# Three RMS norms of an encoder layer rearranged: ones as the stationary operand in halves, squares summed elsewhere, operands made in pieces

## The chip, the core and the metric

The kernel runs on one core of a Trainium2 chip. Five engines work at the same time, each on its own instructions in order: TensorE (PE in the profile; PEld is its loading of weights), VectorE (DVE), ScalarE (ACT), GpSimd (POOL) and SyncE (SP), which here mostly issues DMAs. SBUF holds the tiles, PSUM the results of matmuls, and an instruction waits on semaphores for what it reads or overwrites. The metric is the device time of one execution in microseconds (us), as the median over runs.

## The reference

One layer of a streaming encoder for a prompt of 512 tokens and eight decode streams of 16 tokens (640 columns together, model width 2048). RMS norms stand at four places; the change touches the first and the two inside `merge_and_ffn`.

```python
def rmsnorm(x, g):
    xf = x.astype(jnp.float32)
    y = xf * lax.rsqrt(jnp.mean(xf * xf, axis=-1, keepdims=True) + EPS)
    return (y * g.astype(jnp.float32)).astype(x.dtype)
...
def merge_and_ffn(x, oa, ob, norm_grp_a, norm_grp_b, w_out, norm_ffn, w_gate, w_up, w_down):
    o = jnp.concatenate([rmsnorm(oa, norm_grp_a), rmsnorm(ob, norm_grp_b)], axis=-1)
    x = x + o @ w_out
    h = rmsnorm(x, norm_ffn)
    return x + (jax.nn.silu(h @ w_gate) * (h @ w_up)) @ w_down
...
    qa, ka, va, qb, kb, vb = split_proj(rmsnorm(x, norm_mix) @ w_in)
```

Group A (`oa`) is chunk-band attention of 16 heads of 64 with a learned bias and keys of 8 earlier chunks; group B (`ob`) is sliding-window attention with sinks and rotary keys. Each group's result is 1024 wide and has a norm of its own ahead of its half of `w_out`.

## The kernel before

Activations lie transposed: features on the 128 partitions, the 640 tokens along the row, in two halves of HT = 320. The 2048 features are KT = 16 tiles, a group's result 8 tiles (512 prompt columns, SP in the code, and 128 of decode). A product in fp32 accuracy is made of three matmuls in fp32r (`mm3`, L235 to L237): each operand is split into a high part, written by ACT (L226 for weights, L230 for activations with the norm's gain), and the rest, written by DVE (L227, L231). One `dense` (L247) makes one tile of 128 outputs: for each input tile the two halves times three matmuls, into one pair of PSUM banks (`dn`). Other PSUM results (scores, transposes, sums of norms) take banks from the pool `at`.

A norm's factor depends on the token alone, so it is applied to the result of the product: DVE multiplies the PSUM result by `r_mix` (L412), `r_b` (L1004) or `r_a`. These tiles are 128 x 640 with the same row on every partition. `rstd_steps` (L265) makes them from `ssq`, the sum over tiles of squares: PE sums over the partitions with `ssq` as the stationary operand and a column of ones as the moving one (L273, six columns in all, one for each block of up to 128 tokens), DVE and ACT work out 1/sqrt with a Newton step on 128 x 6 numbers (L275 to L280, ACT's square root with its table at L276), and after a yield PE spreads them over the partitions again (L285, six matmuls against the identity); ACT copies them out of PSUM (L290).

The program's order, as far as the change touches it:
- The start loads `xT` tile by tile with the first pieces of `w_in` (START_CHUNKS) on SP's queue. The gains of the norms come second there (L373) and are read by the first split_gain (L230).
- `input_norm` squares all 16 input tiles on ACT (L389), adds them on DVE (L394), and then runs `rstd_steps`. It runs as a queue beside the first two `dense`, a step at a time as matmuls are emitted; L412 then frees the first `dn` pair.
- Next come group B's heads, and the projections for q, k and v as quartets of Strassen products. In the last quartet (to about 536 us) `release` loads the eight tiles of `ob` and makes group B's operands from them (split_gain), as input tiles become free.
- Then `w_out_b`: 16 `dense` of 8 input tiles, m = 0 to 15. Their matmuls share PE with three queues that the helper `pump` serves in turns: the norm (`norm_b`: seven squares on ACT L302 after a first at L299, added on DVE L303, then `rstd_steps`), group A's heads (scores L425 to L428, exponentials L438, weighted values L464), and the decode of group A (`decode_a`). Once m = 1 is emitted, the norm's queue is run out and `r_b` used. At m = 12 what is left of the queues is run out.
- Group A's results go to memory (`oa_d`) as they are made (`done`, and L730 for decode). `group_operands` (L917) loads them again, splits them, squares them on ACT and adds the squares on POOL: four tiles at m = 12, four after m = 15. Its `rstd` stands behind the first `dense` of `w_out_a`.

Tiles come from lists that are handed on by hand (`get`, `put`), so a tile that is put back earlier or later also moves who waits for it.

## Time and profile before

| what | us |
|---|---|
| runs: median (lowest to highest) | 2544.72 (2541.51 to 2547.5) |
| the profiled execution, whole | 2540.53 |
| its span, first to last instruction | 2538.8 |
| PE busy | 2488.2 |
| DVE busy | 1966.8 |
| ACT busy | 1057.6 |
| POOL busy | 703.2 |

The mean granted TensorE clock is 0.995. An overview by 40 equal slices of some 63 us each; a digit is the busy share in tenths, 9 is 90% or more, and PEclk is the granted clock in tenths of the full one:

```profile
PE   8999999989999999999999999999999999999997
DVE  6666767685567787788888888888889877777797
ACT  5445333355555544344343334334334333333343
POOL 0001211110021133323332332323335433333453
PEclk9999999999999999999999999999999999999998
DMA  6234433467863434444344334334437765666655
```

The first slice holds the start and the input norm, the ninth and tenth (508 to 635 us) the end of the quartets and group B's norm, the twelfth and thirteenth group A's norm and `w_out_a`, and everything after that the feed-forward part, which the change leaves alone.

### The profile page before, as it was taken

What the parts mean: (1) busy time and instruction counts of PE and PEld (TensorE: products, weight loads), DVE (VectorE), ACT (ScalarE), POOL (GpSimd) and SP (SyncE); (2) the same over time, 40 slices, a digit from 0 to 9 for tenths busy, and PEclk for the clock granted to TensorE, in tenths of its full rate; (3) what the DMA queues carried; (4) which work ended last, traced back from release to release, by engine and by line L of the source; (5) the groups of instructions that cost most, each with busy time, mean ns of one, the idle gap of its engine ahead of it and who ended that gap; (6) DMA issues with size and microseconds to landing.
All of it is one profiled execution on the core that took longest, in us unless ns stands there. A gap on an engine that the chain in (4) does not pass through costs nothing.

```text
span 2538.8 us, 44665 instructions
## 1 busy us (share of the span) xinstructions
PE 2488.2 (98%) x17325; PEld 2422.5 (95%) x17325; DVE 1966.8 (77%) x2930; ACT 1057.6 (42%) x1701; POOL 703.2 (28%) x566
## 2 busy tenths in 40 slices
PE   8999999989999999999999999999999999999997
PEld 8898899988899999999999999999999999999997
DVE  6666767685567787788888888888889877777797
ACT  5445333355555544344343334334334333333343
POOL 0001211110021133323332332323335433333453
PEclk9999999999999999999999999999999999999998
DMA  6234433467863434444344334334437765666655
GB/s 197 83 98 131 148 123 127 135 235 244 263 219 139 140 130 138 149 156 134 128 130 146 120 127 144 133 128 131 145 120 247 249 170 165 182 171 172 186 160 183
DMA packets 191604, 401.68 MB, mean 158 GB/s; under 512 B 22496, under 2 KB 83936, under 8 KB 191392
## 3 DMA queue, kind: packets, MB, share of 16 engines
q1 hardware_dynamic: 167056, 344.75, 41.5%
q0 software_dynamic: 23184, 52.77, 7.6%
q8 instruction: 136, 2.23, 0.4%
q10 hardware_dynamic: 1152, 1.31, 0.2%
q14 instruction: 76, 0.62, 0.1%
HBM read 311.14 MB, written 86.87 MB: 157 GB/s over the span
## 4 chain that ended last, share of the span: by engine, by line
PE 87%; DVE 7%; DMA 2%; issue 1%; ACT 1%; POOL 0%; SPq 0%; DVEq 0%; ACTq 0%; POOLq 0%
PE dn L235 18%; PE dn L237 17%; PE dn L236 17%; PE at L235 10%; PE at L236 10%; PE at L237 10%; DVE W L227 2%; PE at L341 2%; PE at L464 1%; DMA W<-w_in 1%; PE at L425 1%; DVE S L793 1%; DMA W<-xT 1%; PE at L713 0%; ACT W L226 0%
## 5 line engine op out<-in xcount | busy, mean ns | idle before, releaser
L226 ACT ACTIVATE W<-W 128x1024 fp32r<-128x1024 f32 (+2 forms) x662 | 640.0, 968 | 1050.5 <-PE dn L236 554.9
L235 PE MATMUL dn<-S,W 128*128 128x320 f32 x3374 | 1055.9, 313 | 10.3 <-ACT W L226 5.1
L237 PE MATMUL dn<-S,W 128*128 128x320 f32 x3374 | 1046.3, 310 | 7.9 <-DVE W L227 7.7
L236 PE MATMUL dn<-S,W 128*128 128x320 f32 x3374 | 1044.7, 310 | 0.3 <-DVE S L227 0.3
L227 DVE TENSOR_TENSOR W<-W,W 128x1024 fp32r<-128x1024 f32 (+2 forms) x662 | 798.0, 1206 | 89.7 <-ACT W L226 85.5
L235 PEld LDWEIGHTS dn<-S,W 128*128 128x128 f32 x3374 | 635.0, 188 | 27.1 <-issue 13.8
L237 PEld LDWEIGHTS dn<-S,W 128*128 128x128 f32 x3374 | 634.4, 188 | 13.4 <-DVE W L227 11.7
L236 PEld LDWEIGHTS dn<-S,W 128*128 128x128 f32 x3374 | 635.1, 188 | 1.1 <-DVE S L227 0.6
L237 PE MATMUL at<-S,W 128*128 128x320 f32 x1834 | 567.4, 309 | 1.2 <-DVE W L227 1.0
L235 PE MATMUL at<-S,W 128*128 128x320 f32 x1834 | 567.6, 309 | 0.9 <-ACT W L226 0.9
L236 PE MATMUL at<-S,W 128*128 128x320 f32 x1834 | 567.0, 309 | 0.0
L774 POOL TENSOR_TENSOR W<-W,W 128x1024 f32<-128x1024 f32 (+2 forms) x84 | 181.3, 2158 | 771.9 <-DVE W L227 617.7
L237 PEld LDWEIGHTS at<-S,W 128*128 128x128 f32 x1834 | 344.5, 188 | 2.2 <-DVE W L227 1.9
L235 PEld LDWEIGHTS at<-S,W 128*128 128x128 f32 x1834 | 344.7, 188 | 1.4 <-ACT W L226 1.4
L236 PEld LDWEIGHTS at<-S,W 128*128 128x128 f32 x1834 | 344.7, 188 | 0.0
L793 DVE TENSOR_TENSOR S<-S,dn 128x320 f32<-128x320 f32 x398 | 182.2, 480 | 76.2 <-PE dn L237 75.7
L783 POOL TENSOR_TENSOR W<-W,W 128x1024 f32<-128x1024 f32 (+2 forms) x84 | 186.5, 2220 | 182.7 <-DVE W L227 136.4
L793 DVE TENSOR_TENSOR S<-S,at 128x320 f32<-128x320 f32 x292 | 138.3, 482 | 96.4 <-PE at L237 94.8
L767 DVE TENSOR_TENSOR W<-W,W 128x1024 f32<-128x1024 f32 (+2 forms) x86 | 119.9, 1394 | 37.7 <-DMA W<-w_gate 26.1
L771 DVE TENSOR_TENSOR W<-W,W 128x1024 f32<-128x1024 f32 (+2 forms) x86 | 97.9, 1139 | 59.1 <-DMA W<-w_up 29.4
L1082 POOL DMA_DIRECT2D S<-act_d x161 | 88.0, 547 | 166.7 <-PE dn L237 80.1
L1146 DVE TENSOR_TENSOR S<-S,half 128x320 fp32r<-128x320 f32 x147 | 119.8, 835 | 1.9
(157 smaller groups left out, 1703.2 us busy)
## 6 DMA issues: line engine op xcount, KB each, us to landing
S<-act_d POOLq DMA_DIRECT2D x161, 320.0 KB, 3.9
W<-w_gate SPq DMA_DIRECT2D x88, 512.0 KB
W<-w_up SPq DMA_DIRECT2D x88, 512.0 KB
W<-w_in SPq DMA_DIRECT2D x66, 512.0 KB
W<-w_down SPq DMA_DIRECT2D x64, 384.0 KB
act_d<-half SPq DMA_DIRECT2D x147, 160.0 KB
act_d<-S SPq DMA_DIRECT2D x147, 160.0 KB
W<-w_down SPq DMA_DIRECT2D x68, 320.0 KB
```

The lines of the kernel that those rows point to most:

```text
L226: self.nc.scalar.activation(hi, src, AF.Identity)
L227: self.nc.vector.tensor_tensor(lo, src, f(hi), ALU.subtract)
L235: mm(out, a[0], b[0], start=first, stop=False)
L236: mm(out, a[0], b[1], start=False, stop=False)
L237: mm(out, a[1], b[0], start=False, stop=last)
L767: nc.vector.tensor_tensor(b12[:, w], b12[:, w], b22[:, w], sub)
L771: nc.vector.tensor_tensor(s6[:, w], b11[:, w], b12[:, w], sub)
L774: eng.tensor_tensor(b11[:, w], b22[:, w], s6[:, w], sub)
L783: eng.tensor_tensor(b21[:, w], b21[:, w], s6[:, w], sub)
L793: add = lambda o, a, b: nc.vector.tensor_tensor(o, a, b, ALU.add)
L1082: nc.gpsimd.dma_start(out=r(sh(t, 2, HT)), in_=r(act_d[which, :, j]))
L1146: nc.vector.tensor_tensor(r(src), src, hi, ALU.subtract)
```

## The change

1. *Start.* The gains are loaded from ACT's own DMA queue as its first instruction, and a small activation on the ones (made by a memset on POOL) stands ahead of all other ACT work. SP loses that issue.
2. *`wide_steps`* takes the place of `rstd_steps` in the input norm and in group B's. PE now has the ones, broadcast to 128 x 128, as the stationary operand and each half of `ssq` as the moving one, so the sum stands on all partitions at once; DVE takes it from PSUM with scale and EPS, ACT makes the square root of 128 x 640, and DVE the reciprocal and the Newton step on two halves of 320 columns. The second visit to PE and ACT's copies are gone.
3. *Group B.* `release` has ACT square each tile of `ob` in place, right behind its split_gain; `norm_b` only adds the eight on DVE.
4. *Group A.* `done` squares each head pair's 512 prompt columns on ACT and adds them on POOL; `sum_decoded` squares the decode columns on ACT, two yields behind their store, and adds them on DVE. `group_operands` makes no squares and runs at m = 12, 13 and 14 for three, three and two tiles; `rstd` follows at m = 14. On PE its first matmul stands 96 matmuls sooner than before, and 25 matmuls instead of 22 stand between its two visits.

```diff
...
+    def wide_steps(self, ssq, dim, out):
+        nc = self.nc
+        tmp = self.get("S")
+        for a in range(2):
+            ps, half = self.bank()[:, :HT], ssq[:, a * HT:a * HT + HT]
+            nc.tensor.matmul(ps, self.ones.to_broadcast([P, P]), half, start=True, stop=True)
+            nc.vector.tensor_scalar(half, ps, 1.0 / dim, EPS, ALU.mult, ALU.add)
+        yield
+        nc.scalar.activation(tmp, ssq, AF.Sqrt)
+        for a in range(2):
+            y, t, v = (x[:, a * HT:a * HT + HT] for x in (out, tmp, ssq))
+            nc.vector.reciprocal(y, t)
+            nc.vector.tensor_tensor(t, y, y, ALU.mult)
+            nc.vector.scalar_tensor_tensor(t, t, -0.5, v, ALU.mult, ALU.mult)
+            nc.vector.scalar_tensor_tensor(y, t, 1.5, y, ALU.add, ALU.mult)
+            yield
+        self.put("S", tmp)
...
-            sq = self.get(lst)
+            own = self.get(lst)
+            sq = own[:, :x.shape[-1]]
             nc.scalar.activation(sq, x, AF.Square)
             (eng or nc.gpsimd).tensor_tensor(ssq, ssq, sq, ALU.add)
-            self.put(lst, sq)
+            self.put(lst, own)
...
     n.ident, mask_b, n.ones = cst[:, :P], cst[:, P:], gains[:, rest:]
+    nc.scalar.dma_start(out=gains[:, :rest], in_=io["consts"][:, P + 257:])
     nc.gpsimd.memset(n.ones, 1.0)
+    nc.scalar.activation(n.small(1), n.ones, AF.Identity)
...
         xr = n.get("S")
         dma(out=xr, in_=io["xT"][:, kt])
-        if kt == 0:
-            dma(out=gains[:, :rest], in_=io["consts"][:, P + 257:])
...
-        for _ in n.rstd_steps({a: [xs[0][:, a * HT:a * HT + HT]] for a in range(2)}, D, r_mix):
-            for _ in range(3):
+        n.put("S", xs[1])
+        for _ in n.wide_steps(xs[0], D, r_mix):
+            for _ in range(2):
                 yield
-        n.put("S", xs[0], xs[1])
+        n.put("S", xs[0])
...
+    ssq_a, summed = [], set()
+    def sum_decoded(o):
+        nc.scalar.activation(o[:, :512], o[:, :512], AF.Square)
+        nc.vector.tensor_tensor(o[:, :256], o[:, :256], o[:, 256:512], ALU.add)
+        out = ssq_a[0][:, SP:]
+        if SP in summed:
+            nc.vector.tensor_tensor(out, out, o[:, :P], ALU.add)
+            nc.vector.tensor_tensor(out, out, o[:, P:2 * P], ALU.add)
+        else:
+            nc.vector.tensor_tensor(out, o[:, :P], o[:, P:2 * P], ALU.add)
+        summed.add(SP)
     def heads_of(kind, p, held, *args):
         def done(ot):
             dma(out=(oa_d if kind is prompt_a else ob_d)[p, :, :SP], in_=ot[:, :SP])
+            if kind is prompt_a:
+                n.add_square(ssq_a[0][:, :SP], ot[:, :SP], 0 not in summed, "S")
+                summed.add(0)
             n.put("S", ot)
...
         dma(out=oa_d[4 * g:4 * g + 4, :, SP:].rearrange("t p c -> p t c"), in_=sh(o_s, 4, P))
-        n.put("W", *three)
+        n.put("W", *three[1:])
+        yield
+        yield
+        sum_decoded(three[0])
+        n.put("W", three[0])
...
-    def group_operands(o_d, gain, ssq, tiles):
+    def group_operands(o_d, gain, tiles):
         own, out = [], []
         for t in tiles:
             o = n.get("S")
             dma(out=o, in_=o_d[t])
             two, hl = pair("S")
             n.split_gain(o, gain[:, t:t + 1], *hl)
-            n.add_square(ssq, o, t == 0, "S")
...
             n.split_gain(raw_b[t], g_b[:, t:t + 1], *hl)
+            nc.scalar.activation(raw_b[t], raw_b[t], AF.Square)
...
     def norm_b():
-        ssq = n.get("S")
-        for t, o in enumerate(raw_b):
-            n.add_square(ssq, o, t == 0, "S", nc.vector)
-            n.put("S", o)
-            yield
-        for _ in n.rstd_steps({a: [ssq[:, a * HT:a * HT + HT]] for a in range(2)}, 1024, r_b):
-            yield
-        n.put("S", ssq)
+        ssq = raw_b[0]
+        for t in range(1, 8):
+            add(ssq, ssq, raw_b[t])
+            if t % 3 == 0:
+                yield
+        yield
+        for _ in n.wide_steps(ssq, 1024, r_b):
+            yield
+        n.put("S", *raw_b)
...
-    r_a, ssq_a, ssq = n.get("S"), n.get("S"), n.get("S")
+    r_a, ssq = n.get("S"), n.get("S")
+    ssq_a.append(n.get("S"))
+    own_a, acts_a = [], []
...
         if m == 12:
             n.drain()
-            own_a, acts_a = group_operands(oa_d, g_a, ssq_a, range(4))
+        if m >= 12:
+            own, out = group_operands(oa_d, g_a, range(3 * (m - 12), min(3 * (m - 12) + 3, 8)))
+            own_a.extend(own)
+            acts_a.extend(out)
+        if m == 14:
+            n.rstd(ssq_a[0], 1024, r_a)
     n.put("S", r_b, *own_b)
-    more = group_operands(oa_d, g_a, ssq_a, range(4, 8))
-    own_a, acts_a = own_a + more[0], acts_a + more[1]
...
-        if i == 0:
-            n.rstd(ssq_a, 1024, r_a)
...
```

The rows below are the order of one engine's instructions in the built program: line, operation, written tile <- read tiles (tile names with a running number), shape. First, the start. SP before, where `gains` stand second and the first 768-column piece of `w_in` behind `cst`:

```order
L371 DMA S_6_84<-xT 128x640
L373 DMA gains<-consts 128x82
L241 DMA W_7_87<-w_in 128x256
L371 DMA S_12_97<-xT 128x640
L241 DMA W_13_99<-w_in 128x256
L371 DMA S_18_109<-xT 128x640
L371 DMA S_24_121<-xT 128x640
L378 DMA cst<-consts 128x128
L379 DMA cst<-consts 128x256
L371 DMA S_27_129<-xT 128x640
L241 DMA W_19_111<-w_in 128x768
L241 DMA W_28_131<-w_in 128x768
```

SP after, with `gains` gone from it and the first 768-column piece ahead of `cst` and the fifth `xT` tile:

```order
L393 DMA S_7_87<-xT 128x640
L241 DMA W_8_89<-w_in 128x256
L393 DMA S_13_99<-xT 128x640
L241 DMA W_14_101<-w_in 128x256
L393 DMA S_19_111<-xT 128x640
L393 DMA S_25_123<-xT 128x640
L241 DMA W_20_113<-w_in 128x768
L398 DMA cst<-consts 128x128
L399 DMA cst<-consts 128x256
L393 DMA S_28_131<-xT 128x640
L241 DMA W_29_133<-w_in 128x768
```

ACT at the same place, before; its first work waits for the gains:

```order
L230 ACT_TABLE_LOAD
L230 ACTIVATE S_10_93<-S_6_84,gains 128x640
L226 ACTIVATE S_8_88<-W_7_87 128x256
L226 ACTIVATE S_14_100<-W_13_99 128x256
L230 ACTIVATE S_16_105<-S_12_97,gains 128x640
L230 ACTIVATE S_22_117<-S_18_109,gains 128x640
```

ACT after, where the table load stands behind the DMA issue, with the small activation on the ones:

```order
L353 DMA gains<-consts 128x82
L355 ACT_TABLE_LOAD
L355 ACTIVATE sm_76<-gains 128x1
L230 ACTIVATE S_11_95<-S_7_87,gains 128x640
L226 ACTIVATE S_9_90<-W_8_89 128x256
L230 ACTIVATE S_17_107<-S_13_99,gains 128x640
L226 ACTIVATE S_15_102<-W_14_101 128x256
L409 ACTIVATE S_7_87<-S_7_87 128x640
```

The table load now belongs to an activation that reads no loaded data.

Second, ACT in the last quartet. S_798 to S_805 before, and S_796 to S_803 after, are the eight tiles of `ob`; L230 is the gain split of one, L226 the split of a quartet's weights. Before:

```order
L226 ACTIVATE W_816_5389<-W_814_5386 128x1024
L230 ACTIVATE S_812_5381<-S_799_5332,gains 128x640
L230 ACTIVATE S_818_5417<-S_800_5334,gains 128x640
L230 ACTIVATE S_820_5421<-S_801_5336,gains 128x640
L230 ACTIVATE S_824_5455<-S_802_5338,gains 128x640
L226 ACTIVATE W_822_5427<-W_791_5266 128x1024
L230 ACTIVATE S_826_5459<-S_803_5340,gains 128x640
L230 ACTIVATE S_831_5494<-S_804_5342,gains 128x640
L226 ACTIVATE W_829_5466<-W_814_5386 128x1024
L226 ACTIVATE W_855_5531<-W_790_5264 128x1024
```

After, with the squares in place (L988) between them:

```order
L226 ACTIVATE W_814_5383<-W_812_5380 128x1024
L230 ACTIVATE S_810_5374<-S_797_5324,gains 128x640
L988 ACTIVATE S_796_5322<-S_796_5322 128x640
L230 ACTIVATE S_816_5411<-S_798_5326,gains 128x640
L230 ACTIVATE S_818_5416<-S_799_5328,gains 128x640
L988 ACTIVATE S_797_5324<-S_797_5324 128x640
L988 ACTIVATE S_798_5326<-S_798_5326 128x640
L226 ACTIVATE W_820_5423<-W_789_5258 128x1024
L988 ACTIVATE S_799_5328<-S_799_5328 128x640
L230 ACTIVATE S_822_5451<-S_800_5330,gains 128x640
L230 ACTIVATE S_824_5456<-S_801_5332,gains 128x640
L226 ACTIVATE W_827_5464<-W_812_5380 128x1024
```

Three squares now stand ahead of the split W_820, and a fourth ahead of W_827. Each square overwrites a tile that DVE's L231 still reads, so it waits for that.

Third, group B's norm, on ACT and PE. ACT before, up to the split of the third block of `w_out_b` (W_955), which stands 30 rows behind that of the second:

```order
L438 ACTIVATE S_852_5527,sm_5838<-S_852_5527,sm_5837 128x128
L438 ACTIVATE S_853_5528,sm_5838<-S_853_5528,sm_5837 128x256
L438 ACTIVATE S_853_5528,sm_5838<-S_853_5528,sm_5837 128x384
L438 ACTIVATE S_852_5527,sm_5838<-S_852_5527,sm_5837 128x512
L573 ACTIVATE S_921_5849<-at_5850 128x512
L573 ACTIVATE S_923_5862<-at_5863 128x512
L673 ACTIVATE S_930_5890,sm_5887<-S_929_5889,sm_5886 128x256
L674 ACTIVATE S_930_5890,sm_5888<-S_929_5889,sm_5886 128x16
L454 ACTIVATE S_946_5946<-at_5941 128x512
L454 ACTIVATE S_948_5959<-at_5954 128x512
L226 ACTIVATE W_955_5975<-W_954_5974 128x1024
```

ACT after, from the split of the second block (W_899) to that of the third (W_948): one head's four exponentials (L459) and two copies stand between them, and one square root with its table.

```order
L226 ACTIVATE W_899_5760<-W_898_5759 128x1024
L301 ACT_TABLE_LOAD
L301 ACTIVATE S_883_5666<-S_796_5322 128x640
L459 ACT_TABLE_LOAD
L459 ACTIVATE S_841_5517,sm_5713<-S_841_5517,sm_5712 128x128
L459 ACTIVATE S_842_5518,sm_5713<-S_842_5518,sm_5712 128x256
L459 ACTIVATE S_842_5518,sm_5713<-S_842_5518,sm_5712 128x384
L459 ACTIVATE S_841_5517,sm_5713<-S_841_5517,sm_5712 128x512
L611 ACTIVATE W_870_5611<-at_5746 128x512
L611 ACTIVATE W_879_5657<-at_5787 128x512
L226 ACTIVATE W_948_5969<-W_947_5968 128x1024
```

PE before, around the first visit of the norm, in the `dense` of m = 1 (`dn_5742`); the second visit (L285) stands 28 rows behind:

```order
L235 MATMUL dn_5742<-S_810_5377,W_903_5744 128x320
L236 MATMUL dn_5742<-S_811_5378,W_903_5744 128x320
L237 MATMUL dn_5742<-S_810_5377,W_904_5745 128x320
L273 MATMUL at_5755<-gains,S_871_5601 128x1 x6
L341 MATMUL at_5775<-cst,S_876_5615 128x128 x4
L235 MATMUL dn_5742<-S_812_5381,W_903_5744 128x320
L236 MATMUL dn_5742<-S_813_5382,W_903_5744 128x320
L237 MATMUL dn_5742<-S_812_5381,W_904_5745 128x320
```

PE after, where the norm's only visit (L298) stands in the `dense` of m = 0, ahead of four score matmuls (L446):

```order
L298 MATMUL at_5667<-S_796_5322,gains 128x320
L298 MATMUL at_5670<-S_796_5322,gains 128x320
L235 MATMUL dn_5576<-S_822_5451,W_863_5578 128x320
L236 MATMUL dn_5576<-S_823_5452,W_863_5578 128x320
L237 MATMUL dn_5576<-S_822_5451,W_864_5579 128x320
L235 MATMUL dn_5576<-S_822_5451,W_863_5578 128x320
L236 MATMUL dn_5576<-S_823_5452,W_863_5578 128x320
L237 MATMUL dn_5576<-S_822_5451,W_864_5579 128x320
L446 MATMUL at_5679<-S_836_5507,S_837_5508 128x256
L446 MATMUL at_5680<-S_836_5507,S_837_5508 128x256
L446 MATMUL at_5685<-S_831_5497,S_832_5498 128x256
L446 MATMUL at_5686<-S_831_5497,S_832_5498 128x256
```

The norm's first work on PE moved up by 34 rows.

More of the change, by code (lines that the diff above doesn't have):

```diff
@@ L1068, in build @@
                 pass
-    n.put("S", r_a, ssq_a, *own_a)
+    n.put("S", r_a, *ssq_a, *own_a)
     n.move("WH", "H", 4)
```

## The prediction

> **What bounds the kernel now.** I read the page first: the busy times, then the chain that ended last by engine.
>
> ```profile
> PE 2488.2 (98%) x17325; PEld 2422.5 (95%) x17325; DVE 1966.8 (77%) x2930; ACT 1057.6 (42%) x1701; POOL 703.2 (28%) x566
> PE 87%; DVE 7%; DMA 2%; issue 1%; ACT 1%; POOL 0%; SPq 0%; DVEq 0%; ACTq 0%; POOLq 0%
> ```
>
> The matmul engine PE is busy for 2488.2 of 2538.8 us, so no more than some 50 us of idle time can be taken out of it, and the rest of a gain must be matmuls that go away. A change to VectorE (DVE) or ScalarE (ACT) pays only where PE waits for them. So I went by stage: busy time in 40-us windows, at the start, around group B's norm (500 to 620) and around group A's (700 to 780). Columns: stretch, length, PE, weight loads, DVE, ACT, POOL, granted clock, DMA share, GB/s.
>
> ```profile
> 0.00:40.00 40.00, 31.64 (x193) 30.23 (x194) 31.42 (x38) 30.67 (x43) 3.01 (x9) 1.00 0.82 261
> 500.00:540.00 40.00, 38.76 (x258) 37.07 (x258) 31.93 (x39) 22.29 (x28) 8.71 (x8) 1.00 0.72 240
> 540.00:580.00 40.00, 34.23 (x247) 30.09 (x250) 25.97 (x89) 22.87 (x60) 4.22 (x11) 0.91 0.62 212
> 740.00:780.00 40.00, 40.00 (x281) 40.00 (x280) 21.00 (x29) 15.17 (x22) 5.35 (x3) 1.00 0.55 182
> ```
>
> Three of the change's places hold idle PE time; group A's norm holds none (40.00 of 40.00). There only PE's own work counts, and that is the same on both sides: squares and operands that are ready sooner end no wait.
>
> **Term 1, the start.** The timeline of the first 16 us:
>
> ```profile
> 0.74 0.40 SPq L371 DMA_DIRECT2D S<-xT  x1
> 1.20 0.41 SPq L373 DMA_DIRECT2D gains<-consts  x1
> 1.65 0.43 SPq L241 DMA_DIRECT2D W<-w_in  x1
> 4.00 1.28 ACT L230 ACT_TABLE_LOAD   x1 [4.00 <-DMA gains<-consts]
> 5.29 0.83 ACT L230 ACTIVATE S<-S,gains 128x640 fp32r<-128x640 f32 x1
> 6.03 0.40 ACT L226 ACTIVATE S<-W 128x256 fp32r<-128x256 f32 x1
> 6.48 0.63 PE L235 MATMUL dn<-S,S 128*128 128x320 f32 x1 [6.48 <-ACT S L226]
> 8.20 0.63 PE L235 MATMUL dn<-S,S 128*128 128x320 f32 x1 [1.09 <-ACT S L226]
> 14.87 0.41 PE L237 MATMUL dn<-S,W 128*128 128x320 f32 x1 [0.62 <-DVE W L227]
> ```
>
> The table load stands on the path only because it waits for the gains. With the dummy activation on the ones it runs from about 1 us and is gone from the path: L230 starts when the gains and xT[0] are in. The gains landed 2.8 us after their issue (1.20 to 4.00); issued first on ACT's queue at about 0.8 they land near 3.6, and xT[0], issued by SP at 0.74, by the same 2.8 about then. L230 then starts near 3.75 instead of 5.29, and the first matmul near 5.0 to 5.2 instead of 6.48: about 1.4. On SP each issue behind the gains moves up by 0.45 (1.20 to 1.65), and the first 768-column chunk passes three issues of some 0.45 each (cst twice and xT[4]); the 0.62 before 14.87 was DVE splitting that chunk late. Together 1.8. Bounds: 0.5 (only the SP issue moves, if data set the pace: DMA share 0.82) to 2.6 (1.28 of table load, 0.62, and 0.7 of the 1.09).
>
> **Term 2, PE's own work in two norms.** The chain of waits at the input norm and at group B's:
>
> ```profile
> 55.99 1.23 PE at L273 x12
> 59.97 1.28 PE at L285 x12
> 554.12 1.23 PE at L273 x12
> 559.66 1.28 PE at L285 x12
> ```
>
> Before, a norm is two visits to PE: six one-column sums (1.23), and six spreading matmuls of 640 columns in all (1.28). After, it is one visit of two 128x320 f32 matmuls, again 640 columns; I take 1.28 for it. Each norm so loses 1.2 of PE work: 2.4 for two. Bounds: 0.8 to 1.4 for each.
>
> At the input norm the wide chain must not be late. PSUM's bank pair is freed by L412, which needs r_mix.
>
> ```profile
> 61.29 0.44 ACT L290 ACTIVATE S<-at 128x320 f32<-128x320 f32 x1 [0.23 <-PE at L285]
> 63.24 0.82 DVE L412 SCALAR_TENSOR_TENSOR S<-dn,S 128x640 f32<-128x640 f32 x1
> 70.92 1.07 ACT W L226
> L277 DVE RECIPROCAL sm<-sm 128x6 f32<-128x6 f32 x4 | 0.7, 187 | 0.3 <-ACT sm L276 0.3
> L678 DVE RECIPROCAL sm<-sm 128x1 f32<-128x1 f32 x16 | 2.5, 159 | 0.2
> L793 DVE TENSOR_TENSOR S<-S,dn 128x320 f32<-128x320 f32 x398 | 182.2, 480 | 76.2 <-PE dn L237 75.7
> ```
>
> No row has a reciprocal of 320 columns. Its low bound is any 320-wide row, 0.48; from 1 to 6 columns the time goes from 159 to 187 ns, 5.6 ns per column, so 320 columns are about 2.0. I take 2.0, as an estimate from the reciprocal's own rows; eight times the per-column price of a 640-wide add (0.82 of L412's kind) would be 3.3, the high bound. Two reciprocals and six plain operations are then 2 x 2.0 + 6 x 0.48 = 6.9 (3.8 to 9.5), behind two PSUM reads of 0.48 and a square root with its table (1.28, and 0.83 like L230). With one PE visit and two ACT copies gone, r_mix comes near 63 instead of 61.7, and L412 ends 2 to 4 later than its 64.06. The next dense is not done before 70.9, so these 7 us cover it: no cost.
>
> The Trainium skill speaks against the wide form: "VectorE: DVE Perf Modes", in its part on the resources of a lane, says that the reciprocal is an iterative divide with a repeat count of 8. At the page's 0.96 GHz that would be about 2.7 us for 320 columns (an estimate from that page), so the chain would take 8.3; the cover above takes it too, so the sum would be the same. No trace here has the wide form yet.
>
> **Term 3, group B's norm and the stalls around it.** PE's gaps there, each with what ended it:
>
> ```profile
> 525.73 0.41 PE L237 MATMUL dn<-S,W 128*128 128x320 f32 x1 [1.24 <-DVE W L227]
> 545.89 0.91 PE L425 MATMUL at<-S,S 64*128 64x256 f32 x4 [0.69 <-DVE sm L428]
> 548.00 1.43 PE L425 MATMUL at<-S,S 64*128 64x256 f32 x4 [1.21 <-DVE sm L428]
> 569.58 0.41 PE L235 MATMUL dn<-S,W 128*128 128x320 f32 x1 [2.50 <-ACT W L226]
> 571.51 0.42 PE L237 MATMUL dn<-S,W 128*128 128x320 f32 x1 [1.38 <-DVE W L227]
> ...
> 548.00:552.00 4.00, 4.00 (x15) 3.35 (x16) 3.90 (x19) 1.61 (x7) 0.42 (x2) 0.57 0.96 348
> 572.00:576.00 4.00, 4.00 (x21) 3.96 (x20) 1.23 (x1) 1.92 (x4) 0.00 (x0) 0.57 0.76 256
> ```
>
> That is 7.0 us of idling, and after the second and the last gap the granted clock falls to 0.57 of full speed over 4 us, 1.7 lost each: up to 3.4. I count 2.5, since some of it falls on short operations. In all 9.5.
>
> What the change does to them, from the order of ACT and DVE:
> - The seven L303 adds leave DVE's stretch of 535 to 549, where they alternate with the score pass L428 for which PE waits (four of 0.81 stand between 542 and 549). The two gaps before 545.89 and 548.00 shrink; but PE's new L298 pair stands between the scores and needs banks from the same pool. Left of 1.9: about 1.8 (0 to 2.5), in two waits.
> - The 2.50 and the 1.38 are one chain: the split L226 of the third w_out_b block stands on ACT behind four heads' exponentials, norm B's two tables and its copies. After, it stands behind one head's; both gaps go.
> - New: ACT's squares in place, in the last quartet. Each must wait until DVE's L231 has read the same tile, and ACT works in order, so the split L226 behind it waits as well:
>
> ```profile
> 519.51 3.83 DVE L231 SCALAR_TENSOR_TENSOR S<-S,gains,S 128x640 fp32r<-128x640 f32 x2
> 523.66 0.87 DVE L231 SCALAR_TENSOR_TENSOR S<-S,gains,S 128x640 fp32r<-128x640 f32 x1
> 520.89 1.04 ACT L226 ACTIVATE W<-W 128x1024 fp32r<-128x1024 f32 x1
> 533.59 4.49 ACT L302 ACTIVATE S<-S 128x640 f32<-128x640 f32 x7
> ```
>
> Those two L231 end at 523.3, and two squares (0.64 each, 4.49 by 7) follow: the split of 520.89 moves to about 524, and PE's gap of 1.24 becomes about 2.0. Bounds: 1.0, if the DVE runs the two earlier, and 4.
>
> Left in the stage: 2.0 + 1.8, and 0.7 for a chance of 4 in 10 of one clock fall of 1.7: 4.5. Term 3 is 4.5 - 9.5 = -5.0 (-8 to 0).
>
> By the Trainium skill, "TensorE: Matmul & The Clock Gate", Part 1, the clock is halved after at least one idle window of about 3.4 us. The rows differ: gaps of 1.21 and of 2.50 with 1.38 were followed by 0.57. By that rule a new gap of 2.0 costs nothing more, and the stage would be 0.7 better; I go by the rows.
>
> **Term 4, group A.** Eight ACT squares of 128x512, POOL adds and the decode squares are spread over 580 to 735, where PE is nearly full:
>
> ```profile
> 580.00:620.00 40.00, 39.46 (x400) 30.83 (x388) 24.04 (x94) 17.91 (x54) 3.65 (x15) 1.00 0.78 265
> 700.00:740.00 40.00, 39.54 (x322) 35.22 (x320) 31.22 (x75) 28.23 (x64) 9.47 (x5) 1.00 0.62 203
> ```
>
> DVE has 24 and 31 of 40 us to do, so they hide mostly; what stands behind a decode square on ACT waits for the store of group A's decoded rows with it, about 1 us once. I take +0.7 (0 to 3); if the cover of the weights read ahead were gone, each square would cost its 0.6. The three pieces of operands at m = 12 to 14 fall into a stretch with PE full, and rstd at 14 comes 96 matmuls sooner than before, with 25 matmuls of cover against 22.
>
> **The sum.** -1.8 - 2.4 - 5.0 + 0.7 = -8.5, against the profiled execution's own 2540.53: 2532.0. That execution lies 4.2 below the median of the runs, 2544.72, so the forecast is 2536.2, called **2536**.
>
> **The rivals.**
> 1. *Given back in place*, about 2541: the stalls of norm B only move. For it: DVE and ACT are fullest just there (31.93 and 22.29 of 40), so a gap taken from one wait finds the next engine late. Then term 3 is 0 and the others give -3.5. Against it: the split moves ahead of three heads' work.
> 2. *The slower side: ACT held behind squares.* All eight squares wait for a slow L231 (1.9), not two of them. Four weight splits of the last quartet stand behind them; each then comes 2.5 late, and each gap may take a clock fall of 1.7 with it: 4 x 4.2 = 16.8 in place of the 2.0 that I count. That is -8.5 + 14.8 = +6.3, or 2551. It decides from about three late splits on (3 x 4.2 = 12.6 against 2.0 + 8.5). Against it: the next L231, at 523.66, took 0.87.
> 3. *The start is set by data.* The first weights and xT land when they land (share 0.82 over 40 us), and term 1 is 0.5: 2537.5; inside the range.
> 4. *More goes*: one wait of 1.5 is all that remains in the stage, and term 1 is full: -2.4 - 8 - 2.6 = -13, or 2531.7.
> 5. *The change doesn't do what it says* for group A: the order shows rstd earlier, yet no wait ends by it. This is in the forecast, whose time it leaves.
>
> **How the numbers follow.** Forecast (with 3) 0.52, rival 1 0.25, rival 2 0.10, rival 4 0.13. A measurement of this kernel can't tell less than 0.2%, 5.1 us, from no change: the line lies at 2539.6. Faster: 0.13 + 0.48 of the forecast's 0.52 + 0.05 = 0.66; slower: 0.07 of rival 2; the same: 0.27. The terms' bounds all at their best give -2.6 - 2.8 - 8 = -13.4, or 2531; all at their worst -0.5 - 1.6 - 0 + 3 = +0.9, or 2546. Below, I add the 3 us by which a run lay off the median; above, rival 2 is left out, with 1 in 10. Range 2528 to 2546.
>
> **What would show it.** First matmul near 5.1 and L227's gap gone near 13 us; two L298 matmuls of some 1.3 us together in each norm, no L273 there; reciprocals of 320 columns at 2.0; no wait for L226 of over 1 us at 565 to 575; a gap of about 2.0 near 524 to 527; PE full at 740 to 780 as before. The forecast falls if several gaps over 1.2 stand between 515 and 540, if the granted clock in 540 to 580 stays at 0.91, or if r_b, late from reciprocals over 2.7, holds L1049 (before L1004).

## The result, and the profile after

| | before | changed |
|---|---|---|
| median of 7 runs, us | 2543.25 | 2535.75 |
| lowest to highest | 2541.51 to 2547.5 | 2531.67 to 2537.58 |
| profiled execution's span | 2538.8 | 2534.9 |

The ratio is 0.9967 (95% interval 0.9956 to 0.9979): 7.5 us faster by the medians, against 8.5 forecast. The two profiled spans differ by only 3.9; where the rest hides is said in the explanation.

The windows of the changed kernel, with the columns of those before:

```profile
0.00:40.00 40.00, 33.19 (x200) 32.11 (x201) 31.92 (x39) 31.66 (x45) 3.57 (x10) 1.00 0.82 265
500.00:540.00 40.00, 38.29 (x248) 37.58 (x246) 31.17 (x37) 22.76 (x28) 7.87 (x7) 0.96 0.69 229
540.00:580.00 40.00, 37.83 (x314) 32.25 (x315) 34.45 (x107) 25.65 (x70) 5.29 (x13) 1.00 0.69 233
740.00:780.00 40.00, 40.00 (x281) 40.00 (x280) 20.66 (x32) 15.69 (x23) 3.48 (x2) 1.00 0.46 155
```

PE gains 1.6 us of work in the first window and 3.6 in the third, where the granted clock went from 0.91 to 1.00; in the second it fell from 1.00 to 0.96. PE is full at 740 to 780, as before.

The timeline at the start of the changed kernel (start, duration, engine, line; in brackets the idle time before and what ended it):

```profile
1.18 1.28 ACT L355 ACT_TABLE_LOAD   x1 [1.18 <-PEq L1453]
4.30 0.83 ACT L230 ACTIVATE S<-S,gains 128x640 fp32r<-128x640 f32 x1 [1.62 <-DMA gains<-consts]
5.49 0.63 PE L235 MATMUL dn<-S,S 128*128 128x320 f32 x1 [5.49 <-ACT S L226]
15.03 0.84 ACT L226 ACTIVATE W<-W 128x768 fp32r<-128x768 f32 x1 [1.08 <-DMA W<-w_in]
15.93 0.41 PE L235 MATMUL dn<-S,W 128*128 128x320 f32 x1 [1.33 <-ACT W L226]
```

The table load is gone from the path and PE starts 1.0 sooner. At 15.93 it waits 1.33 for the second 768-column piece, whose split starts at 15.03; before it started at 14.95. The gains still come only at 4.30, though they are issued first.

The wide form: first the reciprocals as a group (count, total in us, mean in ns), then PE and DVE at the input norm and PE's gaps around group B's, from the timeline:

```profile
L304 DVE RECIPROCAL S<-S 128x320 f32<-128x320 f32 x4 | 8.3, 2117 | 0.8 <-ACT S L301 0.8
```

```profile
54.77 1.24 PE L298 MATMUL at<-S,gains 128*128 128x320 f32 x4
66.38 0.82 DVE L433 SCALAR_TENSOR_TENSOR S<-dn,S 128x640 f32<-128x640 f32 x1
...
525.78 0.42 PE L235 MATMUL dn<-S,W 128*128 128x320 f32 x1 [0.92 <-ACT W L226]
527.12 0.42 PE L237 MATMUL dn<-S,W 128*128 128x320 f32 x1 [0.79 <-DVE W L227]
548.35 1.34 PE L298 MATMUL at<-S,gains 128*128 128x320 f32 x4 [1.40 <-DVE sm L449]
550.87 1.49 PE L446 MATMUL at<-S,S 64*128 64x256 f32 x7 [0.30 <-DVE sm L449]
565.45 0.30 PE L363 MATMUL at<-cst,S 128*128 128x128 f32 x1 [0.48 <-DVE S L466]
```

From 525.78 on, these are all of PE's gaps of 0.3 us and more between 500 and 600. The 2.50 and the 1.38 are gone. The gap ahead of the last quartet's second block is now two of 1.71 together, and one of 1.40 stands before L298.

To compare kernels over the whole span I lay their traces side by side by the same matmul (the n-th at L235): how much earlier (-) or later it starts than in before's profiled execution, in us.

| n-th (time before) | 14th (17) | 107th (61) | 906th (489) | 1052nd (584) | 1289th (770) |
|---|---|---|---|---|---|
| changed | -1.20 | -2.57 | +0.66 | -5.39 | -5.68 |
| start alone | -1.15 | -1.01 | +0.50 | -0.61 | -0.62 |
| input norm alone | -0.13 | -1.75 | +1.39 | +1.51 | +1.48 |
| norm B alone | -0.01 | +0.66 | +2.18 | -5.40 | -0.98 |
| group A alone | +0.05 | +0.99 | +2.45 | +3.27 | +2.79 |
| all but group A | -1.00 | -0.82 | +1.10 | -4.14 | +1.72 |
| all but start and input | -0.05 | -0.05 | +0.37 | -7.22 | -6.85 |

### The profile page after: what moved, and what is told of

Its sections match the earlier page's. It is cut to its first block, busy times and chain, and to the rows that moved or that the text cites. A ratio compares the mean times of both kernels' runs of the same rounds, so it can differ in the third digit from the quotient of the medians.

```text
span 2534.9 us, 44592 instructions
## 1 busy us (share of the span) xinstructions
PE 2485.7 (98%) x17285; PEld 2419.5 (95%) x17285; DVE 1978.0 (78%) x2945; ACT 1057.4 (42%) x1700; POOL 700.3 (28%) x566
## 3 DMA queue, kind: packets, MB, share of 16 engines
q10 hardware_dynamic: 1296, 1.35, 0.2%
## 4 chain that ended last, share of the span: by engine, by line
PE 85%; DVE 8%; DMA 3%; ACT 2%; issue 1%; POOL 0%; SPq 0%; DVEq 0%; ACTq 0%; POOLq 0%
PE dn L235 17%; PE dn L237 17%; PE dn L236 17%; PE at L237 10%; PE at L236 10%; PE at L235 10%; DVE W L227 2%; PE at L363 2%; PE at L485 1%; DVE S L835 1%; PE at L446 1%; ACT S L459 1%; DMA W<-w_in 1%; DVE S L449 1%; DMA W<-xT 1%
## 5 line engine op out<-in xcount | busy, mean ns | idle before, releaser
L226 ACT ACTIVATE W<-W 128x1024 fp32r<-128x1024 f32 (+2 forms) x662 | 639.9, 968 | 1057.5 <-PE dn L236 553.0
L235 PE MATMUL dn<-S,W 128*128 128x320 f32 x3374 | 1055.0, 313 | 10.6 <-ACT W L226 4.8
L227 DVE TENSOR_TENSOR W<-W,W 128x1024 fp32r<-128x1024 f32 (+2 forms) x662 | 799.4, 1208 | 88.0 <-ACT W L226 80.7
L235 PEld LDWEIGHTS dn<-S,W 128*128 128x128 f32 x3374 | 634.9, 188 | 25.5 <-issue 12.2
L235 PE MATMUL at<-S,W 128*128 128x320 f32 x1834 | 567.9, 310 | 1.1 <-ACT W L226 1.1
L235 PEld LDWEIGHTS at<-S,W 128*128 128x128 f32 x1834 | 345.1, 188 | 1.6 <-ACT W L226 1.6
```

The lines of the kernel that those rows point to most:

```text
L226: self.nc.scalar.activation(hi, src, AF.Identity)
L227: self.nc.vector.tensor_tensor(lo, src, f(hi), ALU.subtract)
L235: mm(out, a[0], b[0], start=first, stop=False)
```

## The experiments

Each kernel was timed beside runs of before on the same chip; 5 to 11 runs of each, 22 to 33 of before in a job (medians of before 2542.97, 2543.03 and 2543.06). A ratio compares the runs of one job and need not be the quotient of the medians.

| run | median, us | ratio to before | 95% interval |
|---|---|---|---|
| start alone | 2542.52 | 0.9999 | 0.9990 to 1.0008 |
| input norm alone | 2542.86 | 0.9996 | 0.9988 to 1.0005 |
| norm B alone | 2541.30 | 0.9992 | 0.9983 to 1.0001 |
| group A alone | 2541.31 | 0.9995 | 0.9986 to 1.0004 |
| start and input norm | 2542.00 | 0.9994 | 0.9985 to 1.0003 |
| all but group A | 2541.09 | 0.9992 | 0.9983 to 1.0001 |
| all but start and input | 2536.33 | 0.9972 | 0.9960 to 0.9983 |
| late squares | 2532.42 | 0.9957 | 0.9944 to 0.9971 |
| operands in two pieces | 2534.38 | 0.9964 | 0.9952 to 0.9977 |
| squares in the tail | 2536.67 | 0.9981 | 0.9971 to 0.9990 |
| late squares, late sum | 2543.37 | 1.0005 | 0.9996 to 1.0014 |
| late start | 2533.98 | 0.9970 | 0.9958 to 0.9982 |

**Start alone.** The changed lines of the start, on the kernel before.

```diff
+    nc.scalar.dma_start(out=gains[:, :rest], in_=io["consts"][:, P + 257:])
     nc.gpsimd.memset(n.ones, 1.0)
+    nc.scalar.activation(n.small(1), n.ones, AF.Identity)
...
-        if kt == 0:
-            dma(out=gains[:, :rest], in_=io["consts"][:, P + 257:])
```

> Only the start is changed: gains from ACT's queue, and the activation on the ones. Theory 'the terms add' (the prediction): 1.8 us faster than before, all the way to the end. Theory 'given back': PE runs 1 to 1.5 us ahead up to about 100 us, but is level with before again at 250 us, where a wait at the transposes behind DVE's decode work has grown, and the whole is within 1 us of before. Rival 'the first weights pace it': PE is level with before already at 16 us, since it waits there for the second 768-column piece.

PE is 1.15 ahead at 17 us, so not level there as the rival has it, 1.01 ahead at 61, and 0.50 behind at 489. The time is that of before.

**Input norm alone.** `wide_steps`, used in `input_norm` only.

```diff
-        for _ in n.rstd_steps({a: [xs[0][:, a * HT:a * HT + HT]] for a in range(2)}, D, r_mix):
+        for _ in n.wide_steps(xs[0], D, r_mix):
```

> Only the input norm is changed (wide_steps in it). Theory 'the terms add': PE 1.2 us ahead from 61 us on, and the whole 1.2 us faster. Theory 'given back': 1.2 us ahead at 61 to 110 us, and level with before at 250 us; the whole within 1 us of before. Reciprocals of 320 columns near 2.1 us as in the changed kernel, with the first dense pair freed 4 us later and no PE wait from that.

PE is 1.75 ahead at 61 us and 1.39 behind at 489, and the time is that of before. "Level at 250" missed for these two (0.75 ahead and 0.79 behind), though nothing lasts.

**Norm B alone.** `wide_steps` in `norm_b`, the squares in `release`, the rest as before.

```diff
             n.split_gain(raw_b[t], g_b[:, t:t + 1], *hl)
+            nc.scalar.activation(raw_b[t], raw_b[t], AF.Square)
...
-        for _ in n.rstd_steps({a: [ssq[:, a * HT:a * HT + HT]] for a in range(2)}, 1024, r_b):
+        for _ in n.wide_steps(ssq, 1024, r_b):
```

> Only group B's norm is changed: squares in place in the last quartet, the adds, and wide_steps. Theory 'the terms add': 6.2 us faster (5.0 of waits and 1.2 of PE's work). Theory 'given back' says the same of this part, 5 to 7 us faster, since nothing behind it is paced by anything but PE. Rival 'group A's order makes it': under 3 us, and the waits for L226 near 567 to 571 stay.

Neither theory. From 489 to 584 us this kernel gains 7.6, and from 584 to 770 it gives 4.4 back, with a wait of 2.21 for L227 at 732 us and a granted clock of 0.91 over 720 to 740. The time shows 1.7, not told apart from nothing.

**Group A alone.** Squares in `done` and `sum_decoded`, operands at m = 12 to 14, rstd at m = 14; the rest as before.

```diff
+                n.add_square(ssq_a[0][:, :SP], ot[:, :SP], 0 not in summed, "S")
...
-            n.add_square(ssq, o, t == 0, "S")
```

> Only group A is changed: squares at its results, decode squares, operands in three pieces, rstd at m = 14. Theory 'the terms add': 0.7 us slower (0 to 3). Rival 'group A's order makes it': 3 to 5 us faster, with the waits near 567 to 571 gone or shorter.

No difference that can be told, and its trace still has the waits, 2.50 for L226 at 572 us and 1.03 for L227 at 574: the rival falls. So four parts that each bring at most 1.7 by their medians bring 7.5 together.

**Start and input norm together**, the two diffs above.

> The start and the input norm together, the rest as before. Theory 'the terms add': PE 2.2 to 2.6 us ahead at 61 us and the whole as much faster. Theory 'given back': 2.2 to 2.6 ahead at 61 us, most of it gone at 313 us (its waits for DVE between 85 and 315 us longer by as much), and the whole under 1 us faster.

1.0 by the medians, of 3.0 forecast; the interval allows 3.8 faster to 0.8 slower. PE was 2.90 ahead at 61 us in this trace and 0.37 at 317, so most of it was gone where the theory "given back" has it, but it was 1.25 ahead again at 489: this run alone doesn't decide.

**All but group A**: the changed kernel with group A's part undone.

> The changed kernel without its group A part (group A's squares and operands as before). Theory 'norm B's gain needs group A's part': a wait of about 2 us for L227 near 730 us and a clock fall behind it, as in the run of norm B alone, so 3 to 5 us slower than the changed kernel and 2 to 4 us faster than before. Theory 'the terms add': within 1 us of the changed kernel.

The wait is there. The timeline of DVE, POOL and PE near it:

```profile
728.09 4.32 DVE L231 SCALAR_TENSOR_TENSOR S<-S,gains,S 128x640 fp32r<-128x640 f32 x2
732.33 2.55 DVE L227 TENSOR_TENSOR W<-W,W 128x1024 fp32r<-128x1024 f32 x1
734.80 0.87 DVE L231 SCALAR_TENSOR_TENSOR S<-S,gains,S 128x640 fp32r<-128x640 f32 x1
...
725.91 7.89 POOL L322 TENSOR_TENSOR S<-S,S 128x640 f32<-128x640 f32 x4 [45.26 <-ACT S L321]
...
734.93 0.64 PE L237 MATMUL dn<-S,W 128*128 128x320 f32 x1 [3.56 <-DVE W L227]
```

While POOL adds group A's squares (725.9 to 733.8), DVE's split L231 takes 2.2 each instead of 0.87, and the weights' L227 2.55 where it takes 1.22 without them (at 746), so PE waits 3.56 for that L227. The window from 720 to 740 shows the price:

```profile
720.00:740.00 20.00, 16.44 (x101) 14.71 (x98) 16.00 (x11) 13.55 (x20) 11.23 (x6) 0.84 0.74 247
```

PE is busy for 16.44 of 20.00 at 0.84 of the clock; in the kernel before and in the changed one it is 20.00 at 1.00. From 584 to 770 us this kernel loses 5.9, and by the ratios it is 6.4 slower than the changed kernel (expected 3 to 5).

**All but start and input norm**: the changed kernel with those two undone.

> The changed kernel with the start and the input norm as before (norm B and group A changed). Theory 'given back': within 1 us of the changed kernel, 6 to 7 us faster than before. Theory 'the terms add': 2 to 3 us slower than the changed kernel.

0.6 slower than the changed kernel by the medians, 6.7 faster than before, as "given back" has it. At 61 us its PE is 2.5 behind that of the changed kernel, at 489 us 0.3 ahead of it.

**Late squares.** In the changed kernel, group B's squares are issued together behind the last split of `release`.

```diff
-            nc.scalar.activation(raw_b[t], raw_b[t], AF.Square)
...
+        if which == 6:
+            for x in raw_b:
+                nc.scalar.activation(x, x, AF.Square)
```

> The changed kernel with group B's eight squares issued together behind its last split, so none stands ahead of the second split L226 of the last quartet and two ahead of the third. Theory 'ACT held behind squares': the two waits near 525 and 526 us (0.92 and 0.79 in the changed kernel) become one of about 1.2 for L227, no clock fall at 528, and the whole is 1.5 to 2.2 us faster than the changed kernel. Rival 'DVE's slow L231 sets it': the waits stay at 1.7 and nothing is gained; or the squares delay the first w_out_b split, and the same is lost near 536.

ACT and PE of this kernel:

```profile
520.83 1.05 ACT L226 ACTIVATE W<-W 128x1024 fp32r<-128x1024 f32 x1
...
525.13 0.42 PE L237 MATMUL dn<-S,W 128*128 128x320 f32 x1 [1.23 <-DVE W L227]
```

The split that stood at 524.68 in the changed kernel starts at 520.83 and PE waits 1.23 instead of 1.71; no clock fall follows. This kernel is the fastest of all: 2532.42, 3.3 below the changed one by medians of two jobs, where 1.5 to 2.2 were expected. The two intervals overlap (0.9944 to 0.9971, 0.9956 to 0.9979).

**Operands in two pieces.** The changed kernel, with four tiles at m = 12, four behind m = 15, and rstd behind the first `w_out_a` dense; the squares stay at the results.

```diff
+            own, out = group_operands(oa_d, g_a, range(4))
-        if m >= 12:
-            own, out = group_operands(oa_d, g_a, range(3 * (m - 12), min(3 * (m - 12) + 3, 8)))
...
-        if m == 14:
-            n.rstd(ssq_a[0], 1024, r_a)
```

> The changed kernel with group A's operands in two pieces again (four tiles at m = 12, four behind m = 15) and rstd behind the first w_out_a dense; the squares stay where the change has them. Theory 'the squares in the tail are what norm B's part exposes': no wait for L227 near 730 us, and within 1 us of the changed kernel. Rival 'the size of the piece does it' (eight splits of four tiles ahead of a weight split on ACT and DVE): a wait of 2 us or more near 730, 3 to 5 us slower than the changed kernel.

As fast as the changed kernel, with PE full over 720 to 760. So the size of the pieces, and the early rstd, make no difference that can be told.

**Squares in the tail.** The other half: three pieces, but their squares made in `group_operands` and added on POOL (and `rstd` behind the first `w_out_a` dense again).

```diff
             n.split_gain(o, gain[:, t:t + 1], *hl)
+            n.add_square(ssq_a[0], o, t == 0, "S")
...
```

> The changed kernel with group A's squares in group_operands again (ACT squares, POOL adds in the tail), its operands in three pieces as in the change, rstd behind the first w_out_a dense. Theory 'the squares in the tail': a wait of 1 us or more for L227 at 720 to 735 us, POOL busy there and L231 slow beside it, 2 to 4 us slower than the changed kernel. Rival 'the size of the piece': no such wait, within 1 us of the changed kernel.

POOL, DVE and PE of this kernel:

```profile
726.73 14.70 POOL L323 TENSOR_TENSOR S<-S,S 128x640 f32<-128x640 f32 x7 [44.59 <-ACT S L322]
...
728.92 2.20 DVE L231 SCALAR_TENSOR_TENSOR S<-S,gains,S 128x640 fp32r<-128x640 f32 x1
731.05 2.60 DVE L227 TENSOR_TENSOR W<-W,W 128x1024 fp32r<-128x1024 f32 x1
...
733.70 0.41 PE L237 MATMUL dn<-S,W 128*128 128x320 f32 x1 [0.83 <-DVE W L227]
742.57 0.41 PE L237 MATMUL dn<-S,W 128*128 128x320 f32 x1 [1.16 <-DVE W L227]
```

The waits are there, 2.0 together, without a clock fall, and the ratio 0.9981 lies above the changed kernel's 0.9967 by 3.6 us; the intervals overlap (0.9971 to 0.9990), so the trace carries the verdict more than the time does.

**Late squares, late sum.** The run with late squares, one more yield ahead of `wide_steps` in `norm_b`; the two L298 then stand behind the last four scores.

```diff
         yield
+        yield
         for _ in n.wide_steps(ssq, 1024, r_b):
```

> The run with late squares, with group B's two L298 matmuls one yield later, so behind the last four score matmuls instead of ahead of them. Theory 'PE waits for banks there': the wait of 1.40 before L298 becomes one of about 1.2 before the scores and L298 then waits little, 0 to 0.5 us faster than the run with late squares. Rival 'r_b comes too late': r_b is 1.5 to 2.5 us later, PE waits for the first bank pair near 562 us by 1 to 2 us, and it is as much slower.

ACT, DVE and PE of this kernel:

```profile
568.05 1.05 ACT L226 ACTIVATE W<-W 128x1024 fp32r<-128x1024 f32 x1
...
569.45 1.21 DVE L227 TENSOR_TENSOR W<-W,W 128x1024 fp32r<-128x1024 f32 x1
...
569.15 0.64 PE L235 MATMUL dn<-S,W 128*128 128x320 f32 x1 [2.99 <-ACT W L226]
```

Some 11 slower than with late squares, and all of norm B's gain gone: a wait of 2.99 for L226 at 569 is back, with clock falls at 549 and 569. The bank waits are no smaller either (0.42, 0.47 and 0.93, against 1.40 and 0.29). The rival had the direction, but not the size, nor the place, which is a weight split and not the bank pair. By the traces 6.0 of it stand at 584 us and 9.1 at 770, with a wait of 1.35 at 720. Which step of the changed order costs the rest isn't settled.

**Late start.** The changed kernel with three more activations on the ones ahead of L230.

```diff
+    for fn in (AF.Sqrt, AF.Exp, AF.Sqrt):
+        nc.scalar.activation(n.small(1), n.ones, fn)
```

> The changed kernel with three more small activations on the ones ahead of L230, each with a table load of 1.28 us, so that PE starts some 3 us later than in the changed kernel. They change no result. Theory 'given back' (the stretch from 110 to 315 us is not paced by PE): PE is about 3 us behind the changed kernel at 61 us, under 1.5 us behind at 490 us, and the whole is within 1.5 us of the changed kernel. Theory 'the terms add': 3 us slower than the changed kernel to the end.

ACT and PE of this kernel:

```profile
7.39 0.81 ACT L230 ACTIVATE S<-S,gains 128x640 fp32r<-128x640 f32 x1
8.26 0.94 PE L235 MATMUL dn<-S,S 128*128 128x320 f32 x2 [8.26 <-ACT S L230]
```

PE starts 2.8 later than in the changed kernel, and at the 14th matmul at L235, 17 us, it is only 0.22 behind; the time is that of the changed kernel (0.9970). It missed its purpose: only 0.4 of the delay reached 61 us, so it says nothing of the stretch behind. It tells of the start instead: work of PE that waits for data isn't made sooner by an earlier first matmul.

## Why the prediction was right, and where not

The total was right (2536 forecast, 2535.75 measured), but not because each term was: two were mis-sized, in opposite directions. That the two figures agree to 0.3 is luck: the gain was forecast 1.0 too large, and from 2544.72 for before, the median of three runs, where seven gave 2543.25.

**Term 1, the start (-1.8): too large.** The step that failed is the first matmul 1.4 sooner, with the 0.62 on top. The first matmul came 1.0 sooner, since the gains landed 3.5 after their issue on ACT's queue at 0.74, not 2.8. The 0.62 went, but the second 768-column piece, which no step of the working looked at, sets the pace at 16 us: its wait of 1.33 took their place. Start alone is 1.0 ahead at 61 us; its ratio says 0.3, and by the interval 1.8 can't be excluded (2.5 faster to 2.0 slower). A start 2.8 us later costs nothing. That is the third rival, "the start is set by data", more than my forecast.

The working also left out that PE's first matmuls are slow. In the changed kernel each starts 0.27 after the one before it up to 12.17 us, and 0.15 after it from 12.39 on:

```profile
11.90 0.47 PE L235 MATMUL dn<-S,S 128*128 128x320 f32 x1
12.17 0.39 PE L236 MATMUL dn<-S,S 128*128 128x320 f32 x1
12.39 0.31 PE L237 MATMUL dn<-S,S 128*128 128x320 f32 x1
12.54 0.30 PE L235 MATMUL dn<-S,W 128*128 128x320 f32 x1
```

Every trace has this step, between 9.9 and 14.0 us. The granted clock of 1.00 in the windows doesn't show it, as the clock's records begin only there. So the lead of an earlier first matmul is made at about half the pace: late start's PE was slow for 3.8 us instead of 6.8, and 2.8 behind at the first matmul became 1.3 at the 25th; the wait of 1.33, which it doesn't have, took the rest.

**Term 2, PE's work (-2.4): right on PE, and half of it doesn't last.** L273 and L285 took 2.51 a norm; L298 takes 1.24 and 1.34. From 17 to 61 us the changed kernel gains 1.4. The reciprocal of 320 columns took 2.12 (taken 2.0); L433, L412 before, ends at 67.2 instead of 64.06, and the seven us of cover held. The Trainium skill's count of 8 ("VectorE: DVE Perf Modes", the resources of a lane) made about 2.7 (an estimate from that page); the row says 2.12.

What both terms won by 61 us is not seen at the end. PE has waits for DVE between 80 and 330 us in all kernels; here the largest of each, total and count:

```profile
PE at L341 <- DVE S L610: 1.8, 4, 1.0
PE at L341 <- DVE S L445: 1.4, 2, 0.8
PE at L341 <- DVE S L611: 1.3, 4, 0.7
```

```profile
PE at L363 <- DVE S L649: 2.5, 4, 1.4
PE at L363 <- DVE S L648: 2.3, 4, 0.9
PE at L363 <- DVE S L466: 1.9, 2, 1.1
```

The first is before, the second changed: 4.5 against 6.7 at the same three transposes. All the traces say the same. From the 107th matmul at L235 to the 500th (61 to 306 us), the five kernels with the old input norm take 245.0 to 246.4 us, with 6.8 to 8.1 of it PE idling, and the nine with the new one 247.3 to 248.8, with 8.4 to 9.7. So what the input norm wins is given back there, some 2 us. Why these waits grow wasn't tried.

Whether the start's 1.0 lasts can't be told. Up to group B's norm PE's order is the same in before, norm B alone, group A alone and all but start and input, and they stand at 0, +2.18, +2.45 and +0.37 at 489 us: executions of one order differ by 2.5 there. The times say 1.0 for both terms (start and input norm together) and 0.6 (the changed kernel with and without), each with 2 to 3 us of uncertainty. The spans differ by only 3.9 and not by 7.5 because before's profiled execution lies 2.7 below the median of its runs, and the changed kernel's 1.0 above.

**Term 3, group B (-5.0, and 1.2 of term 2): right.** From the 984th matmul at L235 (524 us) to the 1052nd the changed kernel gains 6.1, against 6.2. Its parts: the split behind the squares 1.71 (2.0 forecast), the bank waits 1.40 and 0.30 (1.8 in all), no stall for L226 (none), 0.48 new, and one clock fall of 1.7 behind the 1.71, which I had counted at 0.4 of one. Rival 2, ACT held behind squares, was real at that size: late squares take 0.5 of the wait and the fall away. It never came near its deciding point of three late splits. That 6.1 meets 6.2 is in part luck: I counted 2.5 for before's two clock falls, which at 1.7 each cost 3.4, and 0.7 for a new one, which cost 1.7. In the five traces with the same waits at 526 us and no fall behind them the same stretch gained 7.6.

**Term 4, group A (+0.7): the wrong sign, once norm B's part is there.** The step that failed is "squares and operands that are ready sooner end no wait", read from a stage in which PE was full before. Alone, group A's part indeed changes nothing that can be told. But norm B's part brings PE forward by 5 to 8 us, against a tail in which DVE's splits are slowed by POOL's adds. In before they are as slow, and PE, coming later, is full all the same (20.00 of 20.00 over 720 to 740):

```profile
731.02 2.60 DVE L227 TENSOR_TENSOR W<-W,W 128x1024 fp32r<-128x1024 f32 x1
```

With norm B's part a wait of 2 to 3.6 us opens there, with a clock fall, and 4 to 6 of norm B's gain are lost (norm B alone; all but group A). Group A's part moves these adds out of the tail, and that lets norm B's gain through. Two pieces are as good as three: it is the squares that matter.

So 3.0 from the start and the input norm became about 1, and 5.5 from norm B and group A became 6.7 (all but start and input).

The Trainium skill, "SBUF — State Buffer", in its part on two separate sides, says that GpSimd and a VectorE operation with two SBUF inputs exclude each other from a shared port pair for the whole of an instruction. The rows above agree: L231 and L227, which read two tiles, took 2.2 and 2.6 beside POOL's adds.

## What to carry to other kernels

An engine that is full in a stage shows no wait there, but may have no slack either: when an earlier stage gets faster, look at which work of the next stage was hidden only by PE being late, and take it out together with the stall. Measure parts of a change alone and left out, both: here each part alone looked like nothing, and leaving group A's out cost most of the gain. A first matmul that starts sooner is worth no more than the next piece of data allows.

## What was unexpected

Behind the same waits the clock fell in some kernels and not in others. After the gaps of 0.92 and 0.79 near 526 us it fell in the changed kernel and in all but group A, and not in the other five traced kernels that have them. What decides is where the gaps lie in time. In each trace the instants at which the granted clock changes are whole multiples of 3.4133 us apart; before's falls start at 548.11, 572.00 and 1968.05, which is 7 and 416 of these after the first. In windows cut at such instants, the changed kernel has both gaps in one window (first rows, with the window behind it), and the kernel without the start and the input norm has one in each of two (second rows):

```profile
524.32:527.73 3.41, 1.70 (x10) 1.18 (x9) 3.41 (x6) 3.41 (x6) 0.02 (x1) 1.00 0.71 229
527.73:531.14 3.41, 3.41 (x15) 3.41 (x14) 3.20 (x4) 2.98 (x5) 0.00 (x0) 0.50 0.81 262
```

```profile
521.98:525.39 3.41, 2.58 (x18) 2.32 (x16) 3.41 (x4) 1.64 (x3) 2.01 (x2) 1.00 1.06 367
525.39:528.80 3.41, 2.52 (x15) 2.27 (x16) 3.41 (x6) 3.41 (x6) 0.00 (x0) 1.00 0.55 168
```

PE busy for 1.70 of 3.41 was followed by 3.41 us at half the clock; 2.58 and 2.52 were not. In all the traces, from the clock's first record to 2500 us, every such window at full clock with PE busy for half of it or less was followed by a fall, and none with 0.63 of it or more; between these there are both.

The Trainium skill, "TensorE: Matmul & The Clock Gate", Part 1, has windows of 3.4 us that run freely, so that the phase of a gap would matter; that agrees. Its condition of a whole idle window doesn't: 1.71 us of idling in 3.41 was enough.

With the new start there is such a place at 16 us as well. In two of the nine traced kernels with it, all but group A and squares in the tail, the slow matmuls ended earliest (9.9 and 10.0 us), PE then waited 2.25 and 2.12 for the second 768-column piece, and the clock fell; in the other seven it waited 1.35 or less and the clock stayed. Here all but group A's:

```profile
13.32:16.73 3.41, 1.16 (x8) 0.91 (x7) 1.68 (x3) 1.59 (x3) 0.02 (x1) 1.00 0.99 381
16.73:20.14 3.41, 3.41 (x15) 3.41 (x14) 3.41 (x6) 3.41 (x6) 0.00 (x0) 0.50 0.98 377
```

It costs 1.7, more than the start's part was seen to gain. No trace without the new start has it.
